# Maxima for softmax from 64-row products, two heads side by side on PE

## The chip, the cores and the metric

The kernel runs on one core of one Trainium2 chip. The metric is the device time of one execution in microseconds (us), the median of several runs. Engines are named as in the profile: PE multiplies matrices, DVE, ACT and POOL work elementwise, SP issues most of the DMAs. PSUM is the memory that PE writes to, in banks of 128 partitions x 512 f32.

## The reference, cut to what matters

One transformer layer on 2048 tokens of width 1024, with 256 context tokens: a retention branch and an attention branch side by side, an output projection, then a feed-forward part. Only the attention is touched:

```
q = rope(rmsnorm(aq))          # 8 heads of 64, 2048 tokens
k = [rmsnorm(ak_ctx), rope(rmsnorm(ak))]   # 2 key heads of 64, 256 + 2048 tokens
s = einsum('bqkgd,bskd->bkgqs', q, k) * 64**-0.5
p = softmax(s, axis=-1)
att = einsum('bkgqs,bskd->bqkgd', p, v)
```

Each query needs its exponentials relative to some number near its greatest score. Any number will do that keeps the exponentials in range, as the sum divides it out again.

## The kernel before, in words

**Split numbers.** Queries and keys are held as two f16 parts each, high and low. `ks` (128 rows: high part of the key in rows 0 to 63, low part in 64 to 127) times the first half of `qr` (the query's high part in both halves of the rows) gives high x high + low x high in one product of 128 rows. `ks2` holds the keys' high part again in 64 rows, and in the other 64 rows constants (`unit`) that pick out three rows of `qr`'s second half: the query's maximum in two parts, and a shift. `ks2` times that second half adds high x low and subtracts the maximum, so that the scores leave PE ready for the exponential.

**Groups and iterations.** The work is cut into 32 groups (`Group`): 16 tiles of 128 queries, two key heads each, four query heads to a group. A group has 18 key tiles of 128. The attention stage runs through iterations k; group n begins its maxima at k = 18 n, and its scores 22 iterations later (`LAG`), so the maxima of one group run beside the scores of another. The first group's maxima are made in the stage before and use `piece` alone.

**One group, before.** `load` fetches `qr` from DRAM with four DMAs. In 18 iterations `piece(i)` (line 172, or 176 for the last 256 keys of two heads) makes the scores' main part for one head and 512 keys, in a buffer `mp` of which PSUM holds two, and one iteration later `maximum` (line 185) reduces it on DVE to one negated maximum per query in `nm`. `least` (line 191) takes the minimum of the five, `turn` (line 196) transposes it on PE into an `mp` buffer, `rows` (line 199, ACT) and `rows2` (line 203, DVE) write it as two f16 rows into `qr`. Then, per iteration, `scores` (lines 209 and 210, into `st`), `exp` (ACT, 215), and for every two key tiles `cast` (ACT, 219), `low` (POOL 226 or DVE 228) and `values` (PE, 242 and 243).

**What sets the order.** The order is written out by hand: `on(k, phase, function)` puts a step into iteration k and a phase, and the phases of an iteration run in the order begin, scores, piece, maximum, early, exp, cast, low, chain, pe, values, late, dma. Each engine takes its instructions in that order. In the phases pe and late stand the retention's products and the output projection (lines 1497 to 1499) of an earlier tile of queries. `more_keys` makes `ks2` in six parts between iterations 19 and 34: on ACT the copy of the keys (line 1244), on DVE the constants (line 1245). SP's DMAs stand in one queue too.

Of the kernel before, what the change touches and what calls it, by code (L numbers as in the profile page):

```python
# [11 lines left out]
F32 = mybir.dt.float32  # L12
# [4 lines left out]
AF = mybir.ActivationFunctionType  # L17
ALU = mybir.AluOpType
AX = mybir.AxisListType
# [3 lines left out]
P = 128  # L23
# [6 lines left out]
NK = NT + NC  # L30
H = 4
CH = 128
HD = 64
# [3 lines left out]
PSHIFT = 8  # L37
EARLY = 1

ROW = 8192.0  # L40
# [10 lines left out]
def bc(ap, shape):  # L51
    return ap.to_broadcast(shape)
# [3 lines left out]
def layer_kernel(ctx: ExitStack, tc: tile.TileContext, a: dict, out: bass.AP):  # L56
    nc = tc.nc
    mm = nc.tensor.matmul
# [4 lines left out]
    ident = const.tile([P, P], F32, name="ident")  # L63
# [73 lines left out]
    ks = kp.tile([P, 2, NK * P], F16, name="ks")  # L137
# [9 lines left out]
    class Group:  # L147
# [7 lines left out]
        def load(self, pool=None, tag="qr", bufs=4):  # L155
            self.qr = (pool or qp).tile([P, 2, 4, P], F16, name="qr", tag=tag, bufs=bufs)
            q = self.qr.rearrange("p x (j e) t -> p x j e t", e=2)
            for e in range(2):
                src = aq_d[self.t][64 * e : 64 * e + 64, :, 2 * self.g : 2 * self.g + 2]
                nc.sync.dma_start(q[:64, :, :, e], src)  # L160
                nc.sync.dma_start(q[64:, 0, :, e], src[:, 0])

        def minima(self, pool):
            tag = f"nm{self.n}" if self.n < EARLY else "nm"
# [13 lines left out]
        def maximum(self, i):  # L178
# [5 lines left out]
                src, dst = m.rearrange("p (e k) -> p e k", e=2), self.nm[:, h, :, 4]  # L184
            nc.vector.tensor_reduce(dst, src, axis=AX.X, op=ALU.max, negate=True)  # L185

        def least(self, mt):
            self.mt = mt
            nm = self.nm.rearrange("p a b c -> p (a b) c")
            for c in (64, 96):  # L190
                nc.vector.tensor_reduce(mt[:, :, c], nm, axis=AX.X, op=ALU.min)

        def turn(self):
# [2 lines left out]
                nc.tensor.transpose(self.m[:, h], self.mt[:, h], ident)  # L196

        def rows(self):
            nc.scalar.activation(self.qr[64:, 1], self.m[64:], AF.Copy, scale=1 / ROW)

        def rows2(self):
            lo = self.qr[96:, 1]
            nc.vector.scalar_tensor_tensor(lo, self.m[96:], 1 / ROW, lo, op0=ALU.mult, op1=ALU.subtract)

        def scores(self, kt):
            ps = self.s[kt] = psS.tile([P, 512], F32, name="st", tag="st")
# [60 lines left out]
    with ExitStack() as st:  # L267
# [5 lines left out]
        op = st.enter_context(tc.tile_pool(name="op", bufs=2, reuse_waits="tile"))  # L273
# [212 lines left out]
        for m in range(2, len(TILES)):  # L486
            q = first_turn(m)
# [740 lines left out]

    ks2 = vp.tile([P, 2, NK * P], F16, name="ks2")
    unit = vp.tile([P, 1], F32, name="unit")  # L1230
    nc.vector.tensor_tensor(unit, ident[:, 64:65], ident[:, 96:97], op=ALU.add)
    nc.vector.tensor_tensor(unit, unit, ident[:, 80:81], op=ALU.add)
# [4 lines left out]
    for mt in mts:  # L1237
        nc.gpsimd.memset(mt, 0.0)

        nc.gpsimd.memset(mt[:, :, 80], PSHIFT * math.log(2.0) * HD**0.5)  # L1240

    def more_keys(g, i):
        s = slice(i * 768, (i + 1) * 768)
        nc.scalar.activation(ks2[:64, g, s], ks[:64, g, s], AF.Copy)
        nc.vector.tensor_copy(ks2[64:, g, s], bc(unit[64:], [64, 768]))

    def bank(i, shape=(P, 4, P)):
        return psX.tile(list(shape), F32, name=f"bank{i}", tag=f"bank{i}")
# [3 lines left out]
    def on(k, phase, fn, *args):  # L1252
        events.setdefault((k, phase), []).append((fn, args))
# [28 lines left out]
    def attention():  # L1282
        for n, g in enumerate(groups):
            k = NK * n
# [3 lines left out]
                on(k + NK, "begin", g.load)  # L1288
            if n >= EARLY:
                on(k - 1, "late", g.minima, sm)  # L1290
                for i in range(NK):
                    on(k + i, "piece", g.piece, i)
                    on(k + i + 1, "maximum", g.maximum, i)
            on(k + NK, "chain", g.least, mts[n % 2])
            on(k + NK + 1, "piece", g.turn)
            on(k + NK + 2, "cast", g.rows)
            on(k + NK + 3, "early", g.rows2)
            k += LAG
            for i in range(NK):
                on(k + i, "scores", g.scores, i)  # L1300
# [901 lines left out]
```

## Time and profile before

| | before |
|---|---|
| median of 3 runs | 2789.3 us (2785.25 to 2796.68) |
| the profiled execution | 2786.0 us, span 2784.2 us |
| PE busy | 2641.8 us (95%) |
| DVE, ACT, POOL busy | 2096.0, 1599.6, 1438.0 us |
| mean granted clock of PE | 0.987 |
| reductions of maxima (L185) | 576, 684 ns each |
| maxima products (L172 and L176) | 512 and 128 |

The profile's lines name an operation by its line in the kernel, the engine, and output<-inputs. In the timeline a row gives the start, the duration, and in brackets how long the engine had been idle and what it waited for. PEld is the loading of weights. A matmul's duration includes its way through the array, and matmuls overlap: the distance between two starts says how much of PE's path one takes. Where the timeline's window ends, a row shows only the instructions that began before it, so the same start can stand there with x1 and x2.

### The profile page before, as it was taken

To read this page: it belongs to the slowest core of one execution; us is meant where nothing else is said; L and a number is where in the kernel's file an instruction comes from. 1 tells how busy PE (TensorE), PEld (TensorE's weight loads), DVE (VectorE), ACT (ScalarE), POOL (GpSimd) and SP (SyncE) were. 2 spreads that over 40 slices of the span, in tenths; PEclk is the share of its full clock that TensorE was granted. 3 is DMA by queue.
4 is the path that set the end of the run, shared out by engine and by line. 5 is a ranking of instruction groups with operands and counts; after the bars stand their busy time and mean duration, and the time that the engine had idled before them with its cause. 6 is when DMAs were issued, how large, how long until landed. Compare 5 with 4: busy or idle time off the path is not lost.

```text
span 2784.2 us, 44980 instructions
## 1 busy us (share of the span) xinstructions
PE 2641.8 (95%) x16768; PEld 1416.1 (51%) x16768; DVE 2096.0 (75%) x3306; ACT 1599.6 (57%) x2736; POOL 1438.0 (52%) x1182
## 2 busy tenths in 40 slices
PE   7999999887999999999899889999999999999997
PEld 3545654454666666666565434444444444444443
DVE  5857677678877777777777577988899956666676
ACT  3633762227877777777787566645554564443442
POOL 2623772465656757686767644454556721111155
PEclk8999999999999999999999999999999999999999
DMA  7478658584112222323222755665657332222223
GB/s 265 130 256 294 218 172 265 161 281 144 55 50 66 69 80 67 97 77 94 71 93 76 257 185 170 201 190 161 201 185 276 128 115 84 84 84 83 83 75 138
DMA packets 275046, 402.51 MB, mean 145 GB/s; under 512 B 107717, under 2 KB 163141, under 8 KB 272522
## 3 DMA queue, kind: packets, MB, share of 16 engines
q1 hardware_dynamic: 274538, 398.57, 44.1%
q8 instruction: 132, 2.16, 0.3%
q10 hardware_dynamic: 288, 1.05, 0.1%
q14 instruction: 88, 0.72, 0.1%
HBM read 294.54 MB, written 105.00 MB: 144 GB/s over the span
## 4 chain that ended last, share of the span: by engine, by line
PE 72%; DVE 11%; DMA 5%; ACT 4%; issue 3%; POOL 3%; SPq 1%; POOLq 0%; DVEq 0%; ACTq 0%
PE pu L1706 6%; PE pu L1707 6%; PE pu L1708 6%; PE pd L1883 6%; PE pd L1885 6%; PE pd L1884 6%; PE pso L650 5%; PE pso L651 5%; PE pso L652 5%; PE o L243 3%; PE mp L172 3%; PE st L210 3%; PE st L209 3%; DVE plo L228 2%; PE o L242 2%
## 5 line engine op out<-in xcount | busy, mean ns | idle before, releaser
L185 DVE TENSOR_REDUCE nm<-mp 128x1 f32<-128x512 f32 (+1 forms) x576 | 390.0, 684 | 161.3 <-PE mp L172 132.1
L215 ACT ACTIVATE p<-st 128x512 f32<-128x512 f32 x576 | 339.0, 599 | 173.7 <-PE st L210 105.9
L226 POOL TENSOR_TENSOR plo<-p,phi 128x1024 f16<-128x1024 f32 x160 | 352.4, 2204 | 166.4 <-ACT phi L219 136.1
L1706 PE MATMUL pu<-hf,w1f 128*128 128x512 f16 x896 | 341.5, 381 | 15.5 <-ACT w L1723 8.4
L1707 PE MATMUL pu<-hf,w1f 128*128 128x512 f16 x896 | 341.4, 381 | 0.0
L1708 PE MATMUL pu<-hf,w1f 128*128 128x512 f16 x896 | 341.1, 381 | 0.0
L219 ACT ACTIVATE phi<-p 128x1024 f16<-128x1024 f32 x288 | 304.0, 1056 | 0.0
L651 PE MATMUL pso<-wlo,h 128*128 128x512 f16 (+1 forms) x816 | 295.7, 362 | 2.0 <-DVE wlo L548 2.0
L650 PE MATMUL pso<-whi,h 128*128 128x512 f16 (+1 forms) x816 | 296.0, 363 | 1.3 <-ACT whi L547 1.3
L652 PE MATMUL pso<-whi,h 128*128 128x512 f16 (+1 forms) x816 | 295.5, 362 | 0.0
L242 PE MATMUL o<-wv,plo 128*128 128x65 f16 x2304 | 234.3, 193 | 17.0 <-POOL plo L226 10.2
L228 DVE TENSOR_TENSOR plo<-p,phi 128x512 f16<-128x512 f32 x256 | 234.6, 917 | 16.3 <-ACT phi L219 15.1
L243 PE MATMUL o<-wv,phi 128*128 128x129 f16 x2304 | 242.0, 220 | 0.0
L242 PEld LDWEIGHTS <-plo 128*128 128x128 f16 x2304 | 205.4, 98 | 61.0 <-POOL plo L226 21.3
L1909 DVE SCALAR_TENSOR_TENSOR acc<-pd,scv,acc 128x512 f32<-128x512 f32 x248 | 183.0, 742 | 55.0 <-PE pd L1885 52.3
L209 PE MATMUL st<-qr,ks 128*128 128x512 f16 x576 | 218.8, 380 | 4.9 <-ACT p L215 4.4
L210 PE MATMUL st<-qr,ks 128*128 128x512 f16 x576 | 218.9, 380 | 0.1
L243 PEld LDWEIGHTS <-phi 128*128 128x128 f16 x2304 | 204.9, 97 | 21.1 <-issue 0.3
L172 PE MATMUL mp<-ks,qr 128*128 128x512 f16 x512 | 195.5, 382 | 21.1 <-DVE nm L185 16.2
L1671 POOL TENSOR_TENSOR w1s<-w1r 128x512 f32<-128x512 f32 x64 | 91.7, 1433 | 232.7 <-ACT w L1745 153.7
L1883 PE MATMUL pd<-w2t,us 128*128 128x512 f16 x496 | 188.0, 379 | 4.4 <-DVE acc L1909 4.4
L1885 PE MATMUL pd<-w2t,us 128*128 128x512 f16 x496 | 188.0, 379 | 0.1
(377 smaller groups left out, 6083.9 us busy)
## 6 DMA issues: line engine op xcount, KB each, us to landing
w2t<-w2f SPq DMA_DIRECT2D x98, 512.0 KB, 4.2
wm<-in_w_ff SPq DMA_DIRECT2D x64, 512.0 KB, 5.0
w1r<-in_w_ff SPq DMA_DIRECT2D x64, 512.0 KB, 4.7
w2f<-w2f SPq DMA_DIRECT2D x98, 256.0 KB, 2.4
wmr<-in_w_mod SPq DMA_DIRECT2D x32, 512.0 KB, 5.2
w2r<-in_w_ff SPq DMA_DIRECT2D x32, 512.0 KB, 4.7
hf<-hp SPq DMA_DIRECT2D x56, 256.0 KB, 3.2
hf<-hf SPq DMA_DIRECT2D x14, 1024.0 KB, 7.1
```

What stands on the lines that cost most here:

```text
L185: nc.vector.tensor_reduce(dst, src, axis=AX.X, op=ALU.max, negate=True)
L226: nc.gpsimd.tensor_tensor(lo, p, hi, op=ALU.subtract)
L242: mm(o[:, : HD + 1], lo[:, i, c], v[:, : HD + 1], start=False, stop=False)
L243: mm(o, hi[:, i, c], v[:, :VW], start=False, stop=last)
L650: mm(self.ps[:, c], hi[:, k], wh, start=k == 0, stop=False)
L651: mm(self.ps[:, c], hi[:, k], wl, start=False, stop=False)
L652: mm(self.ps[:, c], lo[:, k], wh, start=False, stop=k == KT - 1)
L1706: mm(pu[c], whi, hi, start=first and k == 0, stop=False, **more)
L1707: mm(pu[c], whi, lo, start=False, stop=False, **more)
L1708: mm(pu[c], wlo, hi, start=False, stop=k == 3, **more)
L1883: mm(ps, uh, wh, start=first and j == 0, stop=False, **more)
L1885: mm(ps, ul, wh, start=False, stop=j == 1, **more)
```

## The change

The maximum no longer comes from high x high + low x high but from high x high alone, which needs 64 rows. `ks2` is turned round: constants in rows 0 to 63, the keys' high part in 64 to 127, so that `ks` has the high parts in the lower half of PE's rows and `ks2` in the upper half. `qr` is turned round in the same way. `both(j)` issues two products of 64 rows one after the other, head h from rows 0 to 63 and head h + 1 from rows 64 to 127, each for 512 keys and into an `mp` buffer of its own; `maxima(j)` reduces both. `piece` remains for the last 256 keys (i = 8 and 17, 128 rows) and for the first group. The pairs stand in every second iteration, 3 to 17 of the group; `rows2` moves one iteration ahead. The keys' copy into `ks2` is made by six DMAs on SP instead of ACT, all six parts in iteration 18.

```diff
@@ load
-                nc.sync.dma_start(q[:64, :, :, e], src)
-                nc.sync.dma_start(q[64:, 0, :, e], src[:, 0])
+                nc.sync.dma_start(q[64:, :, :, e], src)
+                nc.sync.dma_start(q[:64, 0, :, e], src[:, 0])
@@ after maximum
+        def both(self, j):
+            h, c = j // 4 * 2, slice(j % 4 * 512, (j % 4 + 1) * 512)
+            a, b = self.m[18 + j] = [psS.tile([P, 512], F32, name="mp", tag="mp") for _ in range(2)]
+            mm(a, self.qr[:64, 0, h], ks[:64, self.g, c], start=True, stop=True)
+            mm(b, self.qr[64:, 0, h + 1], ks2[64:, self.g, c], start=True, stop=True)
+
+        def maxima(self, j):
+            for e, m in enumerate(self.m.pop(18 + j)):
+                to = self.nm[:, j // 4, e, j % 4 : j % 4 + 1]
+                nc.vector.tensor_reduce(to, m, axis=AX.X, op=ALU.max, negate=True)
@@ least
-            for c in (64, 96):
+            for c in (0, 32):
@@ rows, rows2
-            nc.scalar.activation(self.qr[64:, 1], self.m[64:], AF.Copy, scale=1 / ROW)
+            nc.scalar.activation(self.qr[:64, 1], self.m[:64], AF.Copy, scale=1 / ROW)
-            lo = self.qr[96:, 1]
-            nc.vector.scalar_tensor_tensor(lo, self.m[96:], 1 / ROW, lo, op0=ALU.mult, op1=ALU.subtract)
+            lo = self.qr[32:64, 1]
+            nc.vector.scalar_tensor_tensor(lo, self.m[32:64], 1 / ROW, lo, op0=ALU.mult, op1=ALU.subtract)
@@ unit and mts: columns 64, 96 and 80 become 0, 32 and 16
...
@@ more_keys
-        nc.scalar.activation(ks2[:64, g, s], ks[:64, g, s], AF.Copy)
-        nc.vector.tensor_copy(ks2[64:, g, s], bc(unit[64:], [64, 768]))
+        nc.sync.dma_start(ks2[64:, g, s], ks[:64, g, s])
+        nc.vector.tensor_copy(ks2[:64, g, s], bc(unit[:64], [64, 768]))
@@ attention
-                for i in range(NK):
-                    on(k + i, "piece", g.piece, i)
-                    on(k + i + 1, "maximum", g.maximum, i)
+                for i in (8, 17):
+                    on(k + i // 9 * 2, "piece", g.piece, i)
+                    on(k + i // 9 * 2 + 1, "scores", g.maximum, i)
+                for j in range(8):
+                    on(k + 2 * j + 3, "piece", g.both, j)
+                    on(k + 2 * j + 4, "scores", g.maxima, j)
             on(k + NK, "chain", g.least, mts[n % 2])
             on(k + NK + 1, "piece", g.turn)
             on(k + NK + 2, "cast", g.rows)
-            on(k + NK + 3, "early", g.rows2)
+            on(k + NK + 2, "low", g.rows2)
@@ where more_keys is placed
-        on(19 + 2 * i, "begin", more_keys, 0, i)
-        on(26 + 4 * i, "late", more_keys, 1, i)
+        on(18, "begin", more_keys, 1, i)
+        on(18, "begin", more_keys, 0, i)
```

In the changed kernel the lines move by 11 or more: `turn` is line 207, `rows` 210, `rows2` 214, the scores 220 and 221, `low` on DVE 239, the values 253 and 254; `both` is 190 and 191, `maxima` 196, `least` 202. Three places show how the order moves.

PE in the middle of a group, two iterations without other work, before (`ks_6842` is how the listing cuts the name of `ks2`):

```order
L209 LDWEIGHTS ks
L209 MATMUL st<-qr,ks 128x512
L210 LDWEIGHTS ks_6842
L210 MATMUL st<-qr,ks_6842 128x512
L172 LDWEIGHTS qr
L172 MATMUL mp<-ks,qr 128x512
L209 LDWEIGHTS ks
L209 MATMUL st<-qr,ks 128x512
L210 LDWEIGHTS ks_6842
L210 MATMUL st<-qr,ks_6842 128x512
L172 LDWEIGHTS qr
L172 MATMUL mp<-ks,qr 128x512
```

and now:

```order
L220 LDWEIGHTS ks
L220 MATMUL st<-qr,ks 128x512
L221 LDWEIGHTS ks_6842
L221 MATMUL st<-qr,ks_6842 128x512
L190 LDWEIGHTS qr
L190 MATMUL mp<-ks,qr 128x512
L191 LDWEIGHTS qr
L191 MATMUL mp<-ks_6842,qr 128x512
L220 LDWEIGHTS ks
L220 MATMUL st<-qr,ks 128x512
L221 LDWEIGHTS ks_6842
L221 MATMUL st<-qr,ks_6842 128x512
```

Two single products, one in each iteration, have become one pair in the first, with full-size products on both sides.

DVE where one group's maxima end and the next one's begin (`nm_6866` is the earlier group's tile, `mp_7168` the buffer of its turn), before:

```order
L185 TENSOR_REDUCE nm_6866<-mp_7102 128x1
L185 TENSOR_REDUCE nm_6866<-mp_7129 128x2
L228 TENSOR_TENSOR plo_7145<-p32_7094,phi_7135 128x512
L191 TENSOR_REDUCE mt1_6850<-nm_6866 128x4 x2
L185 TENSOR_REDUCE nm_7137<-mp_7141 128x1
L228 TENSOR_TENSOR plo_7145<-p32_7094,phi_7135 128x512
L185 TENSOR_REDUCE nm_7137<-mp_7173 128x1
L185 TENSOR_REDUCE nm_7137<-mp_7184 128x1
L203 SCALAR_TENSOR_TENSOR qr_6861<-mp_7168,qr_6861 32x512
L185 TENSOR_REDUCE nm_7137<-mp_7210 128x1
```

and now (the turn's buffer is `mp_7170`):

```order
L196 TENSOR_REDUCE nm_6866<-mp_7128 128x1
L196 TENSOR_REDUCE nm_6866<-mp_7129 128x1
L239 TENSOR_TENSOR plo_7146<-p32_7096,phi_7134 128x512
L202 TENSOR_REDUCE mt1_6850<-nm_6866 128x4 x2
L185 TENSOR_REDUCE nm_7136<-mp_7142 128x2
L239 TENSOR_TENSOR plo_7146<-p32_7096,phi_7134 128x512
L214 SCALAR_TENSOR_TENSOR qr_6861<-mp_7170,qr_6861 32x512
L185 TENSOR_REDUCE nm_7136<-mp_7183 128x2
L196 TENSOR_REDUCE nm_7136<-mp_7211 128x1
L196 TENSOR_REDUCE nm_7136<-mp_7212 128x1
```

The last pair's two reductions stand directly before the minimum of its group; `rows2` stands ahead of piece 17's reduction, and the first pair's follow that.

SP at the start of the attention stage (`qr_6861` are the queries of the second group, `qr_6879` those of the first, `qr_6867` before), now:

```order
L160 DMA qr_6861<-aq15_134 64x4x128
L161 DMA qr_6861<-aq15_134 64x2x128
L1255 DMA ks2_6842<-ks_315 64x768 x6
L160 DMA qr_6879<-aq15_134 64x4x128
L161 DMA qr_6879<-aq15_134 64x2x128
L160 DMA qr_6879<-aq15_134 64x4x128
L161 DMA qr_6879<-aq15_134 64x2x128
```

Before, the rows of L1255 were not there, and the rest stood in the same order: the six copies of the keys have come between the two loads of queries.

More of the change, by code (lines that the diff above doesn't have):

```diff
@@ L1230, in layer_kernel @@
     unit = vp.tile([P, 1], F32, name="unit")
-    nc.vector.tensor_tensor(unit, ident[:, 64:65], ident[:, 96:97], op=ALU.add)
-    nc.vector.tensor_tensor(unit, unit, ident[:, 80:81], op=ALU.add)
+    nc.vector.tensor_tensor(unit, ident[:, 0:1], ident[:, 32:33], op=ALU.add)
+    nc.vector.tensor_tensor(unit, unit, ident[:, 16:17], op=ALU.add)
     nc.vector.tensor_scalar_mul(unit, unit, ROW)
```

2 lines of the change are left out of this document (1 added, 1 removed).

## The prediction

> **What bounds the kernel now.** I read the slices first, then one window over the attention stage, then the order of starts on PE inside it, then the waits.
>
> ```profile
> span 2784.2 us, 44980 instructions
> PE   7999999887999999999899889999999999999997
> 640.00:1546.00 906.00, 854.96 (x8050) 559.96 (x8049) 712.55 (x1238) 704.26 (x1149) 624.04 (x459) 1.00 0.25 78
> ```
>
> The third row is the stage that the change touches: from 640 to 1546 us (906 us) PE has an instruction in flight for 855, DVE is busy 713, ACT 704, POOL 624, and the granted clock is 1.00. PE is nearest to full, but "busy" counts each matmul to its end. What one costs is the distance between starts:
>
> ```profile
> 1000.36 0.38 PE L209 MATMUL st<-qr,ks 128*128 128x512 f16 x1
> 1000.57 0.38 PE L210 MATMUL st<-qr,ks 128*128 128x512 f16 x1
> 1000.79 0.38 PE L172 MATMUL mp<-ks,qr 128*128 128x512 f16 x1
> 1001.00 0.38 PE L1497 MATMUL bank<-wo,rh 128*128 128x512 f16 x1
> ```
>
> Each lasts 0.38 but the next starts 0.215 later, and between these four PE does not pause. So a maxima product (L172) costs 0.215 us of PE's path, not 0.38. An iteration has two score products (0.43), one maxima product (0.215), every second time the values (0.70, from 1010.87 to 1011.57 in the rows of part B), and in 16 of 35 iterations three products of the output projection (0.65). What PE waits for, in the window 640 to 1546:
>
> ```profile
> PE mp L172 <- DVE nm L185: 15.4, 23, 2.6
> PE mp L196 <- DVE mt L191: 2.6, 4, 0.7
> L185 DVE TENSOR_REDUCE nm<-mp 128x1 f32<-128x512 f32 x555 | 375.7, 684 | 154.6 <-PE mp L172 125.5 <-PE mp L176 26.8
> ```
>
> PE waits 18.0 us for reductions of maxima; DVE, idle 154.6 us before them, mostly waits for PE. So in this stage PE sets the pace, with small interruptions, and the change has to be priced in PE's starts.
>
> **The products, part A.** 31 groups (the first group's maxima stand in an earlier stage, unchanged) lose 16 products of 128 rows each and get 8 pairs of 64 rows: 248 pairs, each in place of two products, 0.43 us. If both halves stream together the pair should take about 0.215, which is 53 us less in all. What is to be paid is the change of tile shape: each pair stands alone between full-size matmuls, so PE goes into 64-row tiles and out again 248 times. Before has few such places, and all are f32: L312 (64 rows) and L393 (32 columns). L703 is the control, f32 too but full size.
>
> ```profile
> 259.65 0.38 PE L652 MATMUL pso<-whi,h 128*128 128x512 f16 x1
> 259.86 0.60 PE L703 MATMUL psx<-ident,ys 128*128 128x128 f32 x4
> 260.30 0.38 PE L650 MATMUL pso<-whi,h 128*128 128x512 f16 x1
> ...
> 458.15 0.38 PE L652 MATMUL pso<-whi,h 128*128 128x512 f16 x1
> 458.46 0.27 PE L312 MATMUL psx<-ident,mrow 64*128 64x64 f32 x1
> 458.46 0.46 PE L312 MATMUL psx<-ident,mrow 64*128 64x64 f32 x4
> 458.86 0.39 PE L650 MATMUL pso<-whi,h 128*128 128x512 f16 x1
> ...
> 232.43 0.38 PE L652 MATMUL pso<-whi,h 128*128 128x512 f16 x1
> 232.74 0.62 PE L393 MATMUL mps<-macc,ones 128*32 128x512 f32 x1
> 232.74 1.04 PE L393 MATMUL mps<-macc,ones 128*32 128x512 f32 x2
> 233.71 0.39 PE L650 MATMUL pso<-whi,h 128*128 128x512 f16 x1
> ```
>
> Control: L703 starts 0.21 after L652, its four take (0.60-0.27)/3 = 0.11 each, and L650 starts 0.44 after the first: no gap on either side. L312: it starts 0.31 after L652, so 0.095 late; its four are (0.46-0.27)/3 = 0.063 apart, 0.25 together, yet L650 starts 0.40 later: 0.15 late. In and out: 0.245. L393, one f32 product in two passes 0.42 apart (1.04-0.62), 0.85 together: 1.28 from L652 to L650, less 0.215 and 0.85, leaves 0.215. A visit to another tile shape costs 0.215 to 0.245; I take 0.23.
>
> Do tiles run side by side at all? The 32-column products at the start say so:
>
> ```profile
> 14.82 0.40 PE L341 MATMUL mpm<-wm,cst 128*32 128x256 f32 x1 [1.31 <-DMA wm<-in_w_mod]
> 14.82 0.41 PE L341 MATMUL mpm<-wm,cst 128*32 128x256 f32 x2 [1.31 <-DMA wm<-in_w_mod]
> ```
>
> One takes 0.40, and two on neighbouring tiles end 0.41 after the first start, so the second begins 0.01 to 0.02 later; no pair of 64-row tiles is in the trace. I take it to hold for rows too. A pair then costs 0.215 + 0.015 + 0.23 = 0.46 against 0.43: **+0.03**, and 248 times +7 us (0.01 to 0.05 by the two switch rows: +2 to +12). Outside these rows lie a switch that is free for f16 (0.23 instead of 0.43: -0.20 each, -50) and tiles that run in turn (0.43 + 0.23: +0.23 each, +57). The value stays with the switch rows, since L312 has the same 64x128 tile shape as the pairs.
>
> The Trainium skill, "TensorEngine Tiling (Array Packing)", Key Properties, says that changing the tiling mode, not just the tile, drains TensorE; the 0.095 and 0.15 beside L312, against none beside L703, agree. By that rule alone the gain of the pair is given back at each visit, unless several pairs are put behind one another.
>
> **The waits, part B.** The buffers of PSUM stay two. Now a pair takes both and is followed by two reductions, 2 x 0.684, in the time in which one reduction had to free one buffer. In the middle of a group that leaves room: from pair to pair lie two iterations, at least 0.43 + 0.46 + 0.43 + 0.70 = 2.0 us, and the reductions end 0.4 + 1.37 = 1.8 after the pair when DVE is free. At the turn of a group it does not:
>
> ```profile
> 1010.01 0.38 PE L176 MATMUL mp<-ks,qr 128*128 128x256 f16 x2
> 1010.43 0.69 DVE L185 TENSOR_REDUCE nm<-mp 128x2 f32<-128x512 f32 x1 [0.60 <-PE mp L176]
> 1010.87 0.19 PE L242 MATMUL o<-wv,plo 128*128 128x65 f16 x1
> 1011.03 0.68 DVE L228 TENSOR_TENSOR plo<-p,phi 128x512 f16<-128x512 f32 x1
> 1011.57 0.38 PE L209 MATMUL st<-qr,ks 128*128 128x512 f16 x1
> 1011.63 0.25 DVE L191 TENSOR_REDUCE mt<-nm 128x4 f32<-128x20 f32 x2
> 1012.03 0.63 PE L196 MATMUL mp<-ident,mt 128*128 128x128 f32 x4
> 1013.01 0.59 ACT L199 ACTIVATE qr<-mp 64x512 f16<-64x512 f32 x1
> 1013.80 0.38 PE L172 MATMUL mp<-ks,qr 128*128 128x512 f16 x1 [0.39 <-DVE nm L185]
> 1014.93 0.70 DVE L203 SCALAR_TENSOR_TENSOR qr<-mp,qr 32x512 f16<-32x512 f32 x1
> ```
>
> Three places get tighter. First, the next group's first piece needs the reduction of the last pair's first half, in the same iteration: 0.4 + 0.69 = 1.1 after the pair, while PE, without projection products, is there after 0.46 + 0.43 = 0.89: 0.2 late. Second, the minimum (L191) now stands behind two reductions and a subtraction, 0.69 later than here, where PE reached the turn (L196) 0.15 after it was ready. Third, the first pair needs the turn's bank, so rows (L199), rows2 (L203, moved one iteration ahead) and the reduction of piece 17: by these rows 1012.03 + 0.98 + 0.59 + 0.70 + 0.69 = 1014.99, while PE, through turn (0.44), scores (0.43), piece 17 (0.22), values (0.70) and scores (0.43), would be there at 1014.25: 0.74 late. Behind the waiting pair stand the next scores, and so exp on ACT. Projection products, where they fall there, hide each of these (0.65). Today's rows of the same kind come to 18.0 us; with the longer chain I add two thirds of that, **+12**. Bounds: 0, if later slack takes it up, and 31 x 1.5 = +46, if 0.2 + 0.54 (0.69 less 0.15) + 0.74 is paid in every group.
>
> **The start, part C.** Six copies on ACT leave, six DMAs on SP come, and all six casts of the units on DVE stand together.
>
> ```profile
> L1244 ACT ACTIVATE ks<-ks x6: 827/831/850, 631.5 to 655.8; 64x768 f16<-64x768 f16 x6
> L1245 DVE CAST ks<-unit x6: 557/558/1264, 631.4 to 658.2; 64x768 f16<-64x768 f32 x6
> 635.61 0.59 PE L172 MATMUL mp<-ks,qr 128*128 128x512 f16 x1 [4.69 <-DMA qr<-aq]
> 631.63 0.32 SPq L710 DMA_DIRECT2D qt<-zs  x1
> 636.63 0.62 SPq L161 DMA_DIRECT2D qr<-aq  x1
> DMA to landing us min/median/max: 2.1/2.7/7.2
> 640.09 0.63 PE L209 MATMUL st<-qr,ks 128*128 128x512 f16 x1
> ```
>
> ACT's 6 x 0.83 = 5 us were beside PE's work: nothing. The casts, 5 x 0.56 + 1.26 = 4.1 from 631.4, end before the queries of group 1 land (PE waits till 635.61): hidden; with that cover gone, 3 us. The DMAs stand on SP ahead of group 0's queries, whose last issue is at 636.63; it lands 2.7 later, 639.3, just ahead of the first scores at 640.09. Six issues, 0.32 (the shortest here, SP's L710) to 0.62 each, move that by 1.9 to 3.7; less the 0.8 between 639.3 and 640.09: **+2** (1 to 3). Swapping the halves in the queries' loads, in rows and in rows2 changes no count and no shape.
>
> **The sum.** 7 + 12 + 2 = +21 on the profiled execution's 2786.0 us (span 2784.2 and 1.8 around it) is 2807. That execution lies 3.3 below the median of 2789.3, so I say **2808**, 0.7% above the median. What a measurement of this kernel can tell from no change is about 0.5%, 14 us.
>
> **Rivals.**
> 1. *The switch costs f16 nothing.* The rows with gaps are all f32. Then A is -50; part of B comes back, since PE now waits for DVE sooner: +15, C +2: 2786 - 33 = 2753. Against it: beside L703, f32 too, there is no gap. The Trainium skill, "TensorE: Matmul & The Clock Gate", Part 3, gives packed tiles a span of one matmul and some 4 ns per tile, and no switch: 0.22 for a pair, as in this rival; no run here shows such a pair.
> 2. *All cancels.* Pair 0.44, waits taken up by PE's own slack (51 of 906 us): 2775 to 2792.
> 3. *The turn decides.* The first pair's wait for rows, rows2 and piece 17 is paid in every group: 2786 + 7 + 46 + 2 = 2841. It decides from about 0.5 us per group on. For it: the 0.39 at 1013.80, at the same place. Against: only 23 waits in 31 groups today, and projection products cover many turns.
> 4. *The halves run in turn*, so the change doesn't do what it says: A is +57, with B and C 2857. Against it: L341.
>
> **How the numbers follow.** Forecast, a small loss (2792 to 2825): 0.38, of which 0.17 lies under 2803. Rival 1: 0.22. Rival 2: 0.18 (0.02 of it faster by over 0.5%). Rival 3: 0.14. Rival 4: 0.08. So faster 0.24, same 0.17 + 0.16 = 0.33, slower 0.21 + 0.14 + 0.08 = 0.43. The range takes in rivals 1 to 3: 2752 to 2845; the forecast's own is 2792 to 2825.
>
> **What will show it.** In the changed kernel, look at one pair in the middle of a group: the second half should start within 0.02 of the first, the first some 0.31 after the product before it starts, and the next product 0.33 to 0.37 after the pair. Starts 0.215 apart instead mean rival 1 (no gaps) or, between the halves, rival 4. PE's waits for reductions should come to about 30 us; over 50 is rival 3. The first scores should start near 642. The forecast is wrong if the pairs stand without gaps, or if the waits vanish.

## The result and the profile after

The changed kernel takes 2801.68 us (median; 2799.71 to 2804.66) where the kernel before takes 2790.87 (2785.25 to 2796.68): ratio 1.0035, 95% interval 1.0022 to 1.0049, a loss of 10.8 us between the medians, 9.8 by the ratio. A later comparison (e11 below) gave 1.0029 (1.0018 to 1.0039). The prediction was 2808 us.

The profiled execution took 2803.03 us, 17.0 more than the one of before. Its first two rows, as for before:

```profile
span 2801.2 us, 44958 instructions
PE   7999999887999999999999889999999999999998
```

The stage in question, from the first to the last start of the scores' first product (L209 before, L220 after), is one window over each trace. The columns are the window, its length, the busy times of PE, PEld, DVE, ACT and POOL, the clock, the DMA share and GB/s. Before, and then after:

```profile
640.09:1545.82 905.73, 854.69 (x8049) 559.86 (x8048) 712.46 (x1238) 704.08 (x1149) 623.86 (x459) 1.00 0.25 78
```

```profile
650.20:1564.40 914.20, 862.51 (x8046) 516.63 (x8047) 698.20 (x1232) 698.11 (x1146) 620.87 (x459) 1.00 0.25 77
```

The 17.0 us divide into three. The scores begin 10.1 us later (650.20 against 640.09), most of it work that the change does not touch: a second profile of the unchanged kernel (e8) has them at 646.30. The stage is 8.5 us longer. What follows it is 1.6 shorter. In the stage PE is busy 7.8 us more, and its idle time is what it was: 914.20 - 862.51 = 51.7 against 51.0. So PE did not come to wait more on the whole; the same number of matmuls takes longer to pass. A pair in the middle of a group, from the timeline of after (start, duration, engine, line):

```profile
1002.15 0.38 PE L221 MATMUL st<-qr,ks 128*128 128x512 f16 x1
1002.46 0.09 PEld L190 LDWEIGHTS <-qr 64*128 64x128 f16 x1 [0.42 <-issue]
1002.46 0.39 PE L190 MATMUL mp<-ks,qr 64*128 64x512 f16 x1
1002.47 0.39 PE L191 MATMUL mp<-ks,qr 64*128 64x512 f16 x1
1002.78 0.39 PE L1511 MATMUL bank<-wo,ah 128*128 128x512 f16 x1
```

The two halves do stream together. But the pair starts 0.31 after the product ahead of it, where 0.215 is the usual distance, and the product behind starts 0.31 after the pair. From L221 to L1511 are 0.63; two full-size products would have taken 0.215 x 3 = 0.645. What is won inside the pair is given back at its two edges.

PE's waits for the maxima in after, window 650 to 1565 (total us, times, longest):

```profile
PE mp L207 <- DVE mt L202: 3.5, 6, 1.1
PE mp L176 <- DVE nm L196: 2.6, 11, 0.3
PE mp L191 <- DVE nm L185: 1.9, 8, 0.4
PE mp L190 <- DVE qr L214: 0.8, 2, 0.6
PE mp L191 <- DVE nm L196: 0.5, 2, 0.2
PE mp L190 <- DVE nm L196: 0.3, 2, 0.2
```

The six rows come to 9.6 us, where before had 18.0. As PE's idle time as a whole did not fall, other waits grew by as much; e2 shows which. This view counts only time in which PE has nothing in flight; a second half that starts late while its first half is still streaming is not in it, and matters below.

The start of the stage in after:

```profile
639.25 0.62 SPq L160 DMA_DIRECT2D qr<-aq  x1
641.90 3.82 SPq L1255 DMA_DIRECT2D ks<-ks  x6
647.74 0.62 SPq L161 DMA_DIRECT2D qr<-aq  x1
650.20 0.58 PE L220 MATMUL st<-qr,ks 128*128 128x512 f16 x1 [2.42 <-DMA qr<-aq]
```

and the row of before that answers to the first, which with the first score at 640.09 gives the distance then:

```profile
632.00 0.62 SPq L160 DMA_DIRECT2D qr<-aq  x1
```

From the first issue of queries to the first score: 10.95 us now, 8.09 before, 2.9 more. The six copies hold SP for 3.82 us between the two loads of queries, and PE waits for the second one.

### The profile page after: what moved, and what is told of

It reads as the page before. It is cut to its first block, busy times and chain, and to the rows that moved or that the text cites. A ratio compares the mean times of both kernels' runs of the same rounds, so it can differ in the third digit from the quotient of the medians.

```text
span 2801.2 us, 44958 instructions
## 1 busy us (share of the span) xinstructions
PE 2656.2 (95%) x16768; PEld 1374.4 (49%) x16768; DVE 2087.4 (75%) x3306; ACT 1591.8 (57%) x2730; POOL 1435.5 (51%) x1182
## 4 chain that ended last, share of the span: by engine, by line
PE 74%; DVE 12%; DMA 4%; ACT 3%; issue 3%; POOL 3%; SPq 1%; POOLq 0%; DVEq 0%; ACTq 0%
PE pu L1720 6%; PE pu L1722 6%; PE pu L1721 6%; PE pd L1897 6%; PE pd L1899 6%; PE pd L1898 6%; PE pso L661 5%; PE pso L662 5%; PE pso L663 5%; PE o L254 3%; PE st L220 3%; PE st L221 3%; PE mp L190 2%; PE bank L1511 2%; DVE plo L239 2%
## 5 line engine op out<-in xcount | busy, mean ns | idle before, releaser
L226 ACT ACTIVATE p<-st 128x512 f32<-128x512 f32 x576 | 340.1, 599 | 189.7 <-PE st L221 125.8
L196 DVE TENSOR_REDUCE nm<-mp 128x1 f32<-128x512 f32 x496 | 318.5, 683 | 169.3 <-PE mp L191 166.7
L1720 PE MATMUL pu<-hf,w1f 128*128 128x512 f16 x896 | 341.9, 382 | 14.7 <-ACT w L1737 8.2
L220 PE MATMUL st<-qr,ks 128*128 128x512 f16 x576 | 220.1, 382 | 8.8 <-ACT p L226 5.6
L221 PE MATMUL st<-qr,ks 128*128 128x512 f16 x576 | 219.5, 381 | 0.0
L1897 PE MATMUL pd<-w2t,us 128*128 128x512 f16 x496 | 188.0, 379 | 2.8 <-DVE acc L1923 2.7
L1899 PE MATMUL pd<-w2t,us 128*128 128x512 f16 x496 | 188.0, 379 | 0.4 <-DVE us L1775 0.4
L1898 PE MATMUL pd<-w2t,us 128*128 128x512 f16 x496 | 188.0, 379 | 0.0
```

The costliest lines, as they stand in the source:

```text
L1720: mm(pu[c], whi, hi, start=first and k == 0, stop=False, **more)
L1897: mm(ps, uh, wh, start=first and j == 0, stop=False, **more)
L1898: mm(ps, uh, wl, start=False, stop=False, **more)
L1899: mm(ps, ul, wh, start=False, stop=j == 1, **more)
```

## The experiments

Each ratio is to the kernel before, measured on the same chip beside the experiment. Changes are to the changed kernel ("after") where nothing else is said. A stage below means the same window, from the first to the last first score product.

### e1: the pairs as two full-size products

```diff
-            mm(a, self.qr[:64, 0, h], ks[:64, self.g, c], start=True, stop=True)
-            mm(b, self.qr[64:, 0, h + 1], ks2[64:, self.g, c], start=True, stop=True)
+            mm(a, self.qr[:, 0, h], ks[:, self.g, c], start=True, stop=True)
+            mm(b, self.qr[:, 0, h + 1], ks[:, self.g, c], start=True, stop=True)
```

> The changed kernel with its pairs as two products of 128 rows (high and low parts of the keys), in the same places, buffers and reductions; only the tile shape differs. By the trace of the changed kernel a pair costs PE 0.095 + 0.003 + 0.318 = 0.416 us, two full-size products 0.431. Theory 1 (the switches eat the gain, and nothing more): 248 x 0.015 = 4 us slower than the changed kernel, less some 3 us that f32 products behind a pair lose today: 2800 to 2806. Rival (the drain harms more than the pair's own rows show, since no weights are loaded ahead across it): the loss goes with the tile shape and the time falls to the kernel before's, about 2791.

Measured: 2794.61 us, ratio 0.9996 (0.9988 to 1.0005). Against 1.0035 and 1.0029 for the changed kernel that is 0.33 to 0.39%, 9 to 11 us, for the shape of the products alone. The theory that the edges just cancel the gain falls. The stage of e1:

```profile
651.41:1558.16 906.75, 854.11 (x8047) 559.14 (x8047) 698.05 (x1232) 696.70 (x1146) 619.82 (x459) 1.00 0.25 78
```

Against after's row the stage is 7.5 us shorter, PE's busy time 8.4 us shorter and its idle time 0.9 longer. So the cost is in the passage through PE, not in waits that empty it. Where exactly can be read by comparing what stands behind a pair in both kernels. After, with a product of f32 behind the pair:

```profile
712.19 0.38 PE L221 MATMUL st<-qr,ks 128*128 128x512 f16 x1
712.50 0.39 PE L190 MATMUL mp<-ks,qr 64*128 64x512 f16 x1
712.50 0.39 PE L191 MATMUL mp<-ks,qr 64*128 64x512 f16 x1
712.82 0.49 PE L1398 MATMUL bank<-of,oqf 128*128 128x128 f32 x2
713.15 0.39 PE L1399 MATMUL bank<-sb,oqb 128*128 128x128 f32 x2
```

The same place in e1:

```profile
713.18 0.38 PE L221 MATMUL st<-qr,ks 128*128 128x512 f16 x1
713.40 0.38 PE L190 MATMUL mp<-ks,qr 128*128 128x512 f16 x1
713.61 0.38 PE L191 MATMUL mp<-ks,qr 128*128 128x512 f16 x1
713.83 0.38 PE L1398 MATMUL bank<-of,oqf 128*128 128x128 f32 x2
714.05 0.39 PE L1399 MATMUL bank<-sb,oqb 128*128 128x128 f32 x2
```

From L221 to L1399: 0.96 in after, 0.87 in e1. Up to L1398 after is ahead by 0.02 (0.63 against 0.65), and then loses 0.11: two f32 products behind a pair last 0.49 (0.33 to the next start), behind full-size ones 0.38 (0.22). This I worked out from the starts of all 248 pairs in both traces (medians):

| | after | e1 |
|---|---|---|
| from the product ahead to the pair | 0.312 | 0.216 |
| from the first to the second half | 0.003 | 0.216 |
| from the second half to the next start | 0.316 to 0.319 | 0.216 |
| next start to the one behind, f16 (180 pairs) | 0.227 | 0.216 |
| next start to the one behind, f32 (50 pairs; L1398, L1368, L1389) | 0.213 | 0.109 |
| next start to the one behind, f32 transposes (18 pairs; L1496, L1543) | 0.165 | 0.109 |
| second halves over 0.05 late | 32, 12.2 us | 26, 8.0 us |

A pair with f16 products behind it costs 0.861 from the product ahead to the second start behind, four full-size starts 0.864: nothing, or a gain of 0.5 us over 180 pairs. With f32 products behind it the same stretch is 0.845 in after and 0.757 in e1, a loss of 0.088 in each of 50 places, 4.4 us; with the f32 transposes 0.797 and 0.757, 0.7 us in 18 places. And 4.2 us are lost because the second half, which may now start 0.003 after the first, more often stands before a bank that is not yet reduced, with no product in front of it that covers the delay. One such place in after:

```profile
818.90 0.37 PE L190 MATMUL mp<-ks,qr 64*128 64x512 f16 x1 [0.16 <-DVE nm L196]
819.50 0.37 PE L191 MATMUL mp<-ks,qr 64*128 64x512 f16 x1 [0.23 <-DVE nm L196]
```

The second half starts 0.60 after the first. Together these give 8.8 us (4.4 + 0.7 + 4.2, less 0.5), where PE's busy time differs by 8.4 and the stage by 7.5. That these two are the cause rests on this ledger of two traces, not on a run that takes one of them away.

### e2: the kernel before, with its halves turned round and the six copies by DMA

Before's products and order, with the changed kernel's halves, its DMAs and casts in iteration 18. Against the kernel before this is the following, with the halves turned in `load`, `least`, `rows`, `rows2`, `unit` and `mts` as in the change (left out here).

```diff
-        nc.scalar.activation(ks2[:64, g, s], ks[:64, g, s], AF.Copy)
-        nc.vector.tensor_copy(ks2[64:, g, s], bc(unit[64:], [64, 768]))
+        nc.sync.dma_start(ks2[64:, g, s], ks[:64, g, s])
+        nc.vector.tensor_copy(ks2[:64, g, s], bc(unit[:64], [64, 768]))
...
-        on(19 + 2 * i, "begin", more_keys, 0, i)
-        on(26 + 4 * i, "late", more_keys, 1, i)
+        on(18, "begin", more_keys, 1, i)
+        on(18, "begin", more_keys, 0, i)
```

> The kernel before with the halves of ks2 and of the queries turned round and the six copies as DMAs in iteration 18; products, reductions and their order as before. Theory 1: only the start moves, the scores begin some 3 us later, and it stays lost: 2791 + 3 = 2794. Rival (the delay is taken up later in the attention stage, where PE waits anyway): 2791. Second rival (the turned halves themselves cost, by the lower rows that ACT and DVE now use): more than 2797.

Measured: 2790.57 us, ratio 0.9978 (0.9968 to 0.9988). This part of the change is a gain of 6 us, not a loss of 2; none of the three expectations had a gain. Its stage:

```profile
648.50:1549.64 901.14, 854.73 (x8048) 560.35 (x8049) 704.39 (x1232) 696.52 (x1146) 622.28 (x459) 0.99 0.25 79
```

It starts 2.3 us later, counted from the last product of the stage ahead (18.9 against 16.6), and is then 4.6 us shorter than before's (901.14 against 905.73), all of it within the first 18 key tiles: from the 12th to the 18th score product it takes 7.1 us, before 10.9. PE is busy as long as before (854.7) and idle 46.4 instead of 51.0. Against e1, which differs from it only in the order (pairs in every second iteration, rows2 earlier): 0.9996 - 0.9978 = 0.18%, 5 us, and by the windows 6.2 us of idle time (52.6 against 46.4). That is the price of the order. It is not paid where PE waits for maxima. PE's waits in the two stages, added up from the profile's waits in us (e2 from 649 to 1549, e1 from 652 to 1558):

| what PE waits for | e2, before's order | e1, the new order |
|---|---|---|
| reductions of maxima, the minimum, `rows2` | 14.2 | 8.4 |
| the low parts that `values` needs (DVE and POOL) | 15.6 | 21.5 |
| operands and banks of the other work in the phases pe and late | 10.2 | 14.7 |
| exponentials | 4.2 | 4.7 |

The new order shortens the waits for maxima and lengthens the others by more. Both kernels have full-size products, so the shape has no part in it. Why the others grow no run shows.

### e3: the first group's queries ahead of the six copies

```diff
-                on(k + NK, "begin", g.load)
+                on(17, "dma", g.load)
```

(in the branch for the first group)

> The changed kernel with the first group's queries fetched ahead of the six copies (one iteration earlier on SP's queue). Theory 1: the scores no longer wait for the queries, the 2.9 us of the start come back: 2802 - 3 = 2799. Rival: the copies are now late for the first pair of the second group, which PE meets before the scores; then nothing is won, 2802.

Measured: 2801.91 us, ratio 1.0024 (1.0016 to 1.0033), 1.0035 and 1.0029 without it: 1 to 3 us less, but the intervals overlap, so a gain is not shown. The stage began 1.7 us sooner after the last product ahead of it (17.8 against 19.6), but in its first six key tiles it lost 2.3 us again. The start does move as expected; what it is worth in the whole is not settled.

### e4: the halves of a pair apart

The second half is issued ahead of the iteration's scores, the first half behind them.

```diff
+        def other(self, j):
+            h, c = j // 4 * 2, slice(j % 4 * 512, (j % 4 + 1) * 512)
+            b = self.m[30 + j] = psS.tile([P, 512], F32, name="mp", tag="mp")
             mm(b, self.qr[64:, 0, h + 1], ks2[64:, self.g, c], start=True, stop=True)
...
                 for j in range(8):
+                    on(k + 2 * j + 3, "begin", g.other, j)
                     on(k + 2 * j + 3, "piece", g.both, j)
```

> The changed kernel with the two halves of each pair apart: one ahead of the iteration's two score products, one behind them. Twice the switches, and no half runs beside another. Each half alone should cost 0.095 + 0.215 + 0.10 = 0.41 where the pair costs 0.416: +0.41 us for each of 248. Theory 1 (PE paces the stage, so nearly all of it shows): 2802 + 90 to 102 = 2892 to 2904. Rival (waits of the stage take up much of it, PE is not the bound): under 2855.

Measured: 2884.78 us, ratio 1.0319 (1.0304 to 1.0335), some 79 us above the changed kernel. The rows of one half and the window:

```profile
1000.00 0.38 PE L226 MATMUL st<-qr,ks 128*128 128x512 f16 x1
1000.31 0.39 PE L190 MATMUL mp<-ks,qr 64*128 64x512 f16 x1
1000.62 0.39 PE L225 MATMUL st<-qr,ks 128*128 128x512 f16 x1
...
647.05:1643.43 996.38, 956.97 (x8046) 545.63 (x8047) 693.94 (x1232) 711.32 (x1146) 616.39 (x459) 0.99 0.23 71
```

A half alone has the same two edges (0.31 and 0.31) as a pair. So what costs is the visit to the other shape, not the number of products in it; the halves do share PE, and standing together saves a whole visit, 0.41 us. Of 248 x 0.41 = 102 us the stage shows 82 (996.4 - 914.2): PE's busy time rose by 94.5, and 12.3 of it came out of its idle time. The rival (under 50 us) falls; the theory's 90 to 102 was too much, since it left out that PE has idle time to fill.

### e5: piece 17's reduction ahead of rows2

```diff
-                    on(k + i // 9 * 2 + 1, "scores", g.maximum, i)
+                    on(k + i // 9 * 2 + (i < 9), "scores" if i < 9 else "early", g.maximum, i)
```

> The changed kernel with the reduction of piece 17 one iteration ahead, before rows2 on DVE. In the changed kernel the second half of a group's first pair starts late in 15 of 31 groups, 7.7 us together, because that reduction stands behind rows2, which waits for ACT. Theory (the turn's chain is a real part of the schedule's loss): these 7.7 us go, half or more of it shows in the time: 4 to 8 us under the changed kernel (ratio to before 1.0005 to 1.002). Rival (DVE now waits for piece 17 on PE ahead of rows2, and the first half is as late as the second was): no change, ratio 1.0035.

Measured: 2805.42 us, ratio 1.0028 (1.0016 to 1.0040): not told apart from the changed kernel's 1.0029 and 1.0035. Late second halves are as many and no shorter than in after (32, 13.5 us, worked out as above; at the groups' first pairs 16 with 9.2 us, in after 15 with 7.7). So the one reduction behind rows2 is not what delays the first pair of a group, or what it gives is lost elsewhere; the theory found no support.

### e6: both halves in one buffer of two banks, one reduction for both

```diff
-            a, b = self.m[18 + j] = [psS.tile([P, 512], F32, name="mp", tag="mp") for _ in range(2)]
+            m = self.m[18 + j] = psP.tile([P, 2, 512], F32, name="mp", tag="mp")
+            a, b = m[:, 0], m[:, 1]
...
-            for e, m in enumerate(self.m.pop(18 + j)):
-                to = self.nm[:, j // 4, e, j % 4 : j % 4 + 1]
-                nc.vector.tensor_reduce(to, m, axis=AX.X, op=ALU.max, negate=True)
+            to = self.nm[:, j // 4, :, j % 4]
+            nc.vector.tensor_reduce(to, self.m.pop(18 + j), axis=AX.X, op=ALU.max, negate=True)
```

The last 256 keys of all four heads go into one such buffer too, at the start of the group, and the turn moves to the phase late.

> The changed kernel with the two banks of a pair as one tile and one reduction for both, the last 256 keys of all four heads in one tile too, and the turn at the end of its iteration. Two reductions of 0.683 us become one of perhaps 1.22. Theory (PE's waits for maxima, 17 us at the pairs, come from the length of the reductions): 5 to 12 us under the changed kernel. Rival (with one buffer PE waits for the whole reduction each time, and the later turn is paid at the scores): 5 to 15 us above it.

Measured: 2814.53 us, ratio 1.0061 (1.0049 to 1.0074), slower than the changed kernel. No second half is late any more, but PE's waits (window 640 to 1650) show what took its place; L218 is the turn, L207 the reduction of the last 256 keys:

```profile
PE mp L218 <- DVE nm L207: 19.5, 28, 1.6
```

With one buffer nothing can be written while anything is being reduced: the turn waits in 28 groups for the last 256 keys' reduction. The pairs themselves wait 6.3 us in this run (3.5 in after). As e6 also moves the last 256 keys and the turn, it shows what one buffer costs in this order, not what a single reduction for both halves would be worth by itself.

### e7: the kernel before, with all copies and casts early

Before, on ACT and DVE as they were, but all six parts in iteration 18.

```diff
-        on(19 + 2 * i, "begin", more_keys, 0, i)
-        on(26 + 4 * i, "late", more_keys, 1, i)
+        on(18, "begin", more_keys, 0, i)
+        on(18, "begin", more_keys, 1, i)
```

> The kernel before with all six parts of ks2 in iteration 18, still copied by ACT, halves as before; so no DMA stands ahead of the first group's queries. The kernel before with turned halves gained 4.2 us between its 12th and its 18th score product, where in the kernel before a copy, a cast and two long subtractions on DVE (2.06 and 2.44 us beside POOL's) stand. Theory (copies and casts among the first group's work cost these 4 us): the same gain, and without the 2.7 us at the start: 0.25% under before, ratio 0.9965 to 0.9985. Rival (the gain is a chance of where DVE's subtractions fall beside POOL's, or comes from SP doing the copies): ratio 0.999 or more.

Measured: 2789.60 us, ratio 0.9970 (0.9959 to 0.9981), 8 us faster than before. So the gain of e2 needs neither turned halves nor DMAs in place of ACT; when the parts are made is enough. This version beats both kernels, with the full-size products.

### e8: the kernel before once more

No edit; one profile on the chip of e5 to e7, to see how far two profiles of one kernel lie apart.

> The kernel before once more, for its profile. In the profiles compared, the stage ahead of the attention ends at 623.5 us before and at 630.2 in the changed kernel, though nothing in it was changed but which half of the rows the first group's queries are loaded into. Theory: that is the spread of one execution to the next, and this one ends near 630. Rival: the change moved it, and this one ends near 623.5.

```profile
646.30:1558.27 911.97, 857.68 (x8050) 561.04 (x8049) 719.37 (x1238) 703.96 (x1149) 621.31 (x459) 0.99 0.25 77
```

Measured: 2801.53 us, with the last product of the stage ahead starting at 629.9 us, as the theory said. The attention stage takes 912.0 us where the first profile had 905.7. Read by score products, the 6.2 us come in four steps of 1.2 to 2.4 us, the first two of them within the first 21 key tiles; between the steps the two traces run nearly alike. So the stage of before is known to some 6 us from one profile, and a difference to it that rests on single profiles carries that; the ratios rest on many executions. Part of this may be the chip and not the execution: the medians of this kernel on the chips used here lie between 2790.9 and 2798.0 us, and the stage ahead ends at 629.1 to 632.1 in all eight profiles of e1 to e8, but at 622.3 to 625.9 in the three of e9 to e11, which ran on another chip, with versions of both kernels in either lot. No run separates the two.

### e9 and e10: only ACT's copies early, only DVE's casts early

Before, with `more_keys` split in two. e9 puts the copies on ACT into iteration 18 and leaves the casts, e10 the other way round; the diff is e9's:

```diff
         nc.scalar.activation(ks2[:64, g, s], ks[:64, g, s], AF.Copy)
+
+    def more_units(g, i):
+        s = slice(i * 768, (i + 1) * 768)
         nc.vector.tensor_copy(ks2[64:, g, s], bc(unit[64:], [64, 768]))
...
-        on(19 + 2 * i, "begin", more_keys, 0, i)
-        on(26 + 4 * i, "late", more_keys, 1, i)
+        on(18, "begin", more_keys, 0, i)
+        on(18, "begin", more_keys, 1, i)
+        on(19 + 2 * i, "begin", more_units, 0, i)
+        on(26 + 4 * i, "late", more_units, 1, i)
```

> The kernel before, with only ACT's six copies of the keys (L1244) moved to iteration 18 and DVE's six casts of the units left in their places between iterations 19 and 34. Of the gain of the run in which both were moved (ratio 0.9970, and a stretch from the 12th to the 18th first score product of a group that took 7.0 us where the kernel before took 10.9 and 11.1), theory 1 gives all to ACT's copies: each holds up an exponential by 0.83 us, and with it the subtraction on DVE, which then starts behind POOL's and lasts over 2 us. It says 0.997 (0.996 to 0.998) here, no subtraction on DVE of over 2 us before the 18th score, and 1.000 in the run with DVE's casts alone. Theory 2 gives it to DVE's casts, which stand ahead of the subtractions on DVE itself: 1.000 (0.999 to 1.001) here, and 0.997 in the other run. If both are needed, both runs lie between, near 0.9985.

> The kernel before, with only DVE's six casts of the units (L1245) moved to iteration 18 and ACT's copies of the keys left in their places. Theory 1 (ACT's copies are the cause): ratio 1.000 (0.999 to 1.001), and subtractions on DVE of over 2 us beside POOL's in the first group's scores, as in the kernel before. Theory 2 (DVE's casts are the cause): 0.997 (0.996 to 0.998), and none of over 2 us there. Between them, near 0.9985: both hold up the same chain.

Measured: e9 2787.98 us, ratio 0.9992 (0.9982 to 1.0001); e10 2786.31 us, ratio 0.9977 (0.9967 to 0.9986). Theory 1, which gave the gain to ACT's copies, falls: they give little or nothing, and DVE's casts most of it. What they do to DVE is seen beside POOL's subtraction. Before, in the first group's scores:

```profile
654.94 2.12 POOL L226 TENSOR_TENSOR plo<-p,phi 128x1024 f16<-128x1024 f32 x1 [2.37 <-ACT phi L219]
655.55 2.06 DVE L228 TENSOR_TENSOR plo<-p,phi 128x512 f16<-128x512 f32 x1
657.71 0.60 ACT L215 ACTIVATE p<-st 128x512 f32<-128x512 f32 x1 [1.08 <-DVE plo L228]
661.30 2.12 POOL L226 TENSOR_TENSOR plo<-p,phi 128x1024 f16<-128x1024 f32 x1 [4.23 <-ACT phi L219]
661.53 2.44 DVE L228 TENSOR_TENSOR plo<-p,phi 128x512 f16<-128x512 f32 x1
```

In e9 a cast itself is caught:

```profile
644.15 2.13 POOL L226 TENSOR_TENSOR plo<-p,phi 128x1024 f16<-128x1024 f32 x1
644.16 2.53 DVE L1248 CAST ks<-unit 64x768 f16<-64x768 f32 x1
649.11 2.12 POOL L226 TENSOR_TENSOR plo<-p,phi 128x1024 f16<-128x1024 f32 x1 [2.84 <-ACT phi L219]
649.77 2.02 DVE L228 TENSOR_TENSOR plo<-p,phi 128x512 f16<-128x512 f32 x1
```

and in e10 DVE is ahead of POOL each time:

```profile
651.18 0.68 DVE L228 TENSOR_TENSOR plo<-p,phi 128x512 f16<-128x512 f32 x1
655.54 0.68 DVE L228 TENSOR_TENSOR plo<-p,phi 128x512 f16<-128x512 f32 x1
656.21 2.13 POOL L226 TENSOR_TENSOR plo<-p,phi 128x1024 f16<-128x1024 f32 x1 [2.36 <-DVE plo L228]
660.25 0.68 DVE L228 TENSOR_TENSOR plo<-p,phi 128x512 f16<-128x512 f32 x1
660.82 2.13 POOL L226 TENSOR_TENSOR plo<-p,phi 128x1024 f16<-128x1024 f32 x1 [2.47 <-PE mp L172]
```

In before DVE's subtraction (0.68 us in e10) begins 0.61 us after POOL's and ends 0.55 after POOL has ended: 655.55 + 2.06 = 657.61 against 654.94 + 2.12 = 657.06. In e10 it begins 0.67 ahead of POOL's and is done in 0.68. The reductions of maxima queue behind it on DVE, and the exponentials on ACT wait 1.08 us for it. In e10 from the 12th to the 18th score product it takes 7.7 us, in e9 and in before 10.9.

### e11: the changed kernel once more

> The changed kernel as it is, on the chip of these runs, for a second profile of it: the kernel before showed 905.7 and 912.0 us from the first to the last first score product in two profiles. If the loss to the run with full-size pairs (914.2 against 906.7 us) is the pairs' own, PE's busy time in that stretch is again about 862 us against 854, whatever the idle time does, and the time is again 1.0035 (1.002 to 1.005) of the kernel before. If the two profiles compared so far differed by chance, the busy time lies near 855 to 858, and the ratio near 1.000 to 1.002.

```profile
645.14:1559.12 913.98, 862.42 (x8046) 516.61 (x8047) 698.19 (x1232) 697.71 (x1146) 620.19 (x459) 1.00 0.25 77
```

Measured: 2799.88 us, ratio 1.0029 (1.0018 to 1.0039). The stage (913.98 us) and PE's busy time in it (862.42) are those of the first profile to 0.3 us. The cost of the shape, 8.3 us more busy time than in e1, is not a chance of one trace. The scores start at 645.14 here, 5 us sooner than in the first profile of the same kernel: so much of the later start there was not the change's (see e8).

## Why the prediction was right, and where its steps were not

The time (2801.7 for 2808) and the sign (a small loss) are right; the terms are so only in part. B and C were put too high, by 7 and 8 us, and A too low by 2 to 4, so the sum was twice the loss that was measured. That it still lay near is partly luck: all the terms are small beside 2790 us, and the sign rests on A, whose size came out of costs that the sum did not have.

| term | predicted | measured |
|---|---|---|
| A, the products' shape | +7 | +9 to +11 (after less e1) |
| B, the order and the waits | +12, by waits for maxima | +5 (e1 less e2), by other waits |
| C, the copies | +2 | -6 (e2 less before) |
| sum | +21 | +8 to +10; directly, after less before, +10.8 |

The measured terms are steps of one chain from after to before, so their sum is the whole difference again and does not check the split.

**A.** The mechanism held: the halves run side by side, a visit to the other shape costs as much as the second product saves, and this holds for f16 as for the f32 rows from which I took it. The gap on the way in is 0.096 where L312 gave 0.095; on the way out 0.10 where L312 gave 0.15. So the pair itself is a little cheaper than said (0.861 for 0.864, where the sum had 0.03 more than two products), and the term came out near by luck, because of two costs that it did not have: 0.04 to 0.09 for f32 products behind a pair, and second halves before a bank that is still being read. The Trainium skill, "TensorEngine Tiling (Array Packing)", Key Properties, has the drain at each change of mode, and both edges of L190 and L191 agree. The Trainium skill, "TensorE: Matmul & The Clock Gate", Part 3, has 4 ns from tile to tile, and the 0.003 us agree; its span without a price for the change does not hold for a pair that stands alone: 0.22 as an estimate by the page, 0.41 to 0.42 in the trace.

**B** has the wrong size and the wrong path. The step that failed is "with the longer chain I add two thirds of that" to today's 18 us: PE's waits for reductions fell to 9.6 us, where I said about 30. The three places that I named do get tighter: the first pair of a group has a late second half in 15 of 31 groups (7.7 us), the turn waits 3.5 us for the minimum instead of 2.6, and piece 8 or 17 waits in 11 places. But the sum was made as if today's waits stayed and new ones came on top, while in the new order most of the waits of single products (15.4 us in before) went away. That is the order's doing and not the shape's, since it shows between e2 and e1 too (14.2 to 8.4 us). I read it as DVE having two iterations' time for two reductions. The 5 us that B did cost were paid in waits that the prediction had no term for: for the low parts before `values`, and in the other work of the phases pe and late (e2's table). So B's sign was right for a reason that it did not name.

**C** failed in its sign. The six DMAs do delay the first scores as was said (by 2.9 us; +1 to +3). But I priced only what the new place of the copies and casts costs. The old place of ACT's copies was put down as "beside PE's work: nothing", and e9 (0.9992) shows little more; for the old place of DVE's casts the sum had no term at all. Four of DVE's casts lay within the first group's scores and pushed its subtractions behind POOL's; taking them out is worth 6 us (e10). Work taken from an engine with idle time was not priced; by the rows of e9 and e10 what it changed is the order in which DVE and POOL come to their subtractions.

**The rivals.** Rival 1 (the switch is free) falls with the 0.31 on both sides of each pair. Rival 2 (all cancels) names nearly what a quiet pair does, but the time is 10 us beyond it, and e1 shows that it is not nothing. Rival 3 (the turn decides) falls with 9.6 us of waits, and e5 moved nothing. Rival 4 falls with the 0.003 us between the halves, and e4 shows what it would have cost. Of the signs that were to show it, the distance between the halves and the gap ahead of the pair were as said; the gap behind it was 0.32 instead of 0.33 to 0.37, the waits 9.6 instead of 30, and the first scores, put near 642, started at 650.2 and 645.1, mostly for the stage ahead of them.

## What to carry to other kernels

A product that needs half of PE's rows is not half the price: at 512 columns of f16 a visit to the smaller tile shape cost 0.2 us, one whole product, so by these prices halves would pay only where several pairs follow one another, which takes PSUM buffers for all of them; no run here tried that. When work is moved, price its old place too: what stood behind it on the same engine, and what the other engines do in that moment. And an engine with idle time is not free to use where it shares something with another one: here casts of 0.56 us on DVE at the wrong moment, four of them among the first scores, cost the kernel 6 us. Last, a wait that shrinks is not time won: the waits for maxima fell by 8 us here and PE's idle time did not.

## What the runs showed of the hardware that I had not expected

- **The weights of a product of another shape are not loaded ahead.** The load of L190 starts together with its matmul (1002.46 both, and within 0.005 us in 243 of 248 pairs) and lasts 0.09; between full-size products the load of L221 starts 0.21 ahead of its matmul. The gap of 0.096 is about as long as the load, but in the rows it lies ahead of the load too; whether it is the load's or the drain's, no run separated.
- **Short f32 products behind a visit lose more**: two of 128 columns that cost 0.22 start to start cost 0.33 behind a pair, in all 50 places, beside the gap itself, and 0.27 where they are transposes (18 places). The f16 products behind the other pairs have 512 columns, so no run separates the type from the length.
- **DVE and POOL take turns.** Of 42 subtractions that begin on DVE in before while POOL's L226 runs, 36 end 0.54 to 0.56 us after it, whether they began 0.04 or 2.2 us into it. In the 32 places where DVE's begins first and still runs when POOL's begins, it is POOL's that is longer: it ends 1.98 to 2.12 us after DVE's, and lasts up to 2.65 us for 2.13. The Trainium skill, "SBUF — State Buffer", section "SBUF: two separate sides", calls the port pair that both share an exclusive lock, held for the whole instruction by whichever starts first; these rows agree. It may also be behind the steps between two profiles of one kernel, since hundredths of a microsecond can decide who is first and the loser pays up to 2 us; this I read from such rows, and no run held the order fixed.
